# Norms of latents and latent keys by one float32 product over 512 tokens in a two-layer decoder trunk

## The chip, the cores and the metric

One core of one Trainium2 chip runs the whole program in one launch. The metric is the time of the run on the device in microseconds (us), where less is better.

## What is computed

The reference is a trunk of two layers (`D_MODEL` 1024, 512 tokens, float32). A layer mixes tokens by latent attention (MLA, 4 heads) and by stick-breaking attention (4 heads), gates and merges the two, and ends with a gated MLP. The change touches the root-mean-square norms of MLA:

```python
def rms_norm(x, g):
    x32 = x.astype(jnp.float32)
    y = x32 * lax.rsqrt(jnp.mean(x32 * x32, axis=-1, keepdims=True) + EPS)
    return (y * g.astype(jnp.float32)).astype(x.dtype)
...
        q = (rms_norm(q_lat, g_q_lat[l]) @ w_uq[l]).reshape(b, s, MLA_HEADS, QK_HEAD_DIM)
        kv = (rms_norm(kv_lat, g_kv_lat[l]) @ w_ukv[l]).reshape(b, s, MLA_HEADS, QK_NOPE_DIM + V_HEAD_DIM)
        k_nope, v_mla = kv[..., :QK_NOPE_DIM], kv[..., QK_NOPE_DIM:]
        k_rope_h = jnp.broadcast_to(k_rope[:, :, None, :], (b, s, MLA_HEADS, QK_ROPE_DIM))
        k = jnp.concatenate([k_nope, k_rope_h], axis=-1)
        q = rms_norm(q, g_q_head[l])
        k = rms_norm(k, g_k_head[l])
```

There are two norms of latents in a layer (256 query features, 128 key-value features) and one norm of the keys for each of four heads: six in a layer, twelve in all, that the change rewrites. The norms of the queries of each head and those of the residual stream stay as they were.

## The kernel before, in words

Features lie along the 128 partitions and the 512 tokens along the columns, so a norm needs a sum over partitions, which a product with ones gives. A weight product is three products of `fp32r` operands (`mm3`: high by high, high by low, low by high), each a 128x128 block of weights against 512 columns of activations. `split` makes such a pair of parts from a float32 tile: a copy on ScalarE, a difference on VectorE.

The program is first listed in the order of the data flow (`Program.add`), with an estimated duration for each instruction. `Program.order` then simulates the engines: each takes the most urgent instruction whose operands and memory are there. The result is a fixed order for each engine, and each engine works through its own order without overtaking. Urgency is the place in the data flow plus a bias. A list of `fills` (24 products each: projections of stick-breaking heads, and gates) serves to keep TensorE at work while the norms and softmaxes run on ScalarE and VectorE: two of them are listed ahead of `latents` with a low urgency (`BIAS_F`), the others come out of `weave`, one for every four steps of the two attentions.

A norm before (`rsqrt_cols`, then `across`): `sums` takes four products, each with a 128x128 block of squares as weights and one column of ones as the moving side, into a [128 tokens, 4] corner of a PSUM bank. Six operations follow on [128, 4] tiles (Ln and Exp on ScalarE, four on VectorE, a Newton step among them). `across` then brings the factor back into every partition by four products, a spread column as weights against the identity. In `latents` VectorE reads that bank directly; for the keys in `mla_proj` ScalarE copies it to `rks` first. The sum of squares of the shared rotary key is taken once a layer by four products of 64 rows (`rsum`), and each head adds it on its [128, 4] tile.

In layer 0 a wide form, `norm_wide`, serves the norm of the input: one float32 product of a 128x128 block of ones with 512 columns gives the sum in every partition, and Ln, Exp and four VectorE operations work on 128x512 tiles.

```python
            r = across(rsqrt_cols(sq, div, 0))          # latents
        rks = slot()                                    # mla_proj
        act(rks, across(rsqrt_cols(sqk, QK, 0, rsum)), AF.Copy)
```

Of the kernel before, what the change touches and what calls it, by code (L numbers as in the profile page):

```python
# [13 lines left out]
ALU = mybir.AluOpType  # L14
# [17 lines left out]
# columns of the packed per-feature vectors  # L32
# [11 lines left out]
class View:  # L44
    """a part of a tile that gets its memory when the order of the program is known"""
# [48 lines left out]
class Program:  # L94
    """Instructions in the order of the data flow; run() picks the order of issue: each engine takes the
    most urgent instruction whose operands and memory are there, by estimated durations."""
# [13 lines left out]
    def add(self, eng, name, cost, table=None, writes=(), reads=(), alt=None, **kw):  # L110
        o = Op()
        o.alt, o.taken = alt, False
        o.eng, o.name, o.kw, o.cost, o.table = eng, name, kw, cost, table
        o.seq = len(self.ops)
        o.prio = o.seq + self.bias
        o.succ, o.slots, o.need = [], [], set()
        for v, w in [(v, False) for v in reads] + [(v, True) for v in writes]:
            t = v.t
            whole = self.tags[t.tag]["psum"]
            for q, qw, qp, qc in t.log:  # L120
                if not (w or qw) and (not whole or q.eng == eng):
                    # two engines do not read one bank of PSUM at a time
                    continue
                if whole or (qp[0] < v.p[1] and v.p[0] < qp[1] and qc[0] < v.c[1] and v.c[0] < qc[1]):
                    if q is not o:
                        o.need.add(q)
            if w and not whole:
                t.log = [e for e in t.log
                         if not (v.p[0] <= e[2][0] and e[2][1] <= v.p[1] and v.c[0] <= e[3][0] and e[3][1] <= v.c[1])
                         or e[0] is o]  # L130
            t.log.append((o, w, v.p, v.c))
            if not t.users or t.users[-1] is not o:
                t.users.append(o)
            if t not in o.slots:
                o.slots.append(t)
        self.ops.append(o)

    def order(self):
# [44 lines left out]
        # the tensor engine's clock halves after a mostly idle window  # L183
# [22 lines left out]
        while events:  # L206
# [19 lines left out]
            for name, e in engines.items():  # L226
                while e["free"] <= time:
# [16 lines left out]
                    # a far more urgent instruction that is about to be ready goes first  # L244
# [22 lines left out]
            # an engine that is still busy looks again when its instruction ends  # L267
# [35 lines left out]
# tiles of features around a norm that are worked in halves of the tokens  # L303
# [14 lines left out]
# steps of the later adaLN products beside each kind of unit  # L318
# [3 lines left out]
class Unit:  # L322
    """both parts of the weights of one step: eight blocks of 128 columns, in two halves"""
# [10 lines left out]
def trunk_kernel(ctx, tc, keys, xT, wstream, wada, cols, cvec, pos, freqs, out):  # L334
# [14 lines left out]
    # ------------------------------------------------------------ instructions  # L349
# [3 lines left out]
    def act(o, i, func, scale=None, bias=None, accum=None, alone=False):  # L353
# [18 lines left out]
        if accum is None and not alone and func in (AF.Copy, AF.Identity):  # L372
            # a copy, scaled and shifted: VectorE can do it too
            akw = dict(out=o, in0=i, scalar1=1.0 if scale is None else scale, scalar2=bias, op0=ALU.mult)
            if bias is not None:
                akw["op1"] = ALU.add
            alt = ("dve", "tensor_scalar", 66 + (1.041 if is_psum(i) or is_psum(o) else 0.52) * o.n
                   + 60 * (len(reads) - 1), akw)
# [21 lines left out]
    def mm(o, w, r, start, stop, skip=False):  # L400
        n = o.n
        # a short product does not hide the load of the next weights
        cost = max(n / 2.4, 107.0) if r.dt == F32R else max(4 * n / 2.4, 215.0)
        kw = dict(out=o, lhsT=w, rhs=r, start=start, stop=stop)
        if skip:
            kw["skip_group_check"] = True
        R.add("pe", "matmul", cost + 3, None, [o], [w, r], **kw)
# [7 lines left out]
    # ------------------------------------------------------------ constants  # L415
# [39 lines left out]
    for n in range(2):  # L455
        # the row in every partition
# [6 lines left out]
    def make_masks():  # L463
# [4 lines left out]
        masks["causal"] = rounded(scr)          # [q, k]: k <= q stays  # L468
        select(scr, zer, ALU.is_gt, NEG, 1, -1)
        masks["strict"] = rounded(scr)          # [k, q]: k < q stays  # L470
        masks["neg"] = rounded(negm)
        select(scr, negm, ALU.is_ge, 0.0, -1, 1)
        masks["tri"] = rounded(scr)             # [j', j]: -1 where j' >= j

    # ------------------------------------------------------------ norms
    def sums(sq):
        """[128 tokens, blocks]: the sums over the rows"""
# [6 lines left out]
    def rsqrt_cols(sq, div, eps, more=None):  # L484
        """[128 tokens, blocks] of 1 / sqrt((sum over the rows + more) / div + eps), with a Newton step"""
        t = sums(sq)
        n = t.n
        if more is not None:
            u = small(n)
            tt(u, t, more, ALU.add)  # L490
            t = u
# [9 lines left out]
    def across(col):  # L501
        """[128, tokens] with the value of its token in every row"""
# [5 lines left out]
    def split(src):  # L508
        """src as the sum of two parts that one pass each carries exactly"""
# [5 lines left out]
    def square(acc, k, x, c=slice(0, S)):  # L515
        """adds the square of feature tile k to the sum"""
# [10 lines left out]
    def norm_wide(acc):  # L527
        """the same in fewer steps, with more work for each"""
        ps = bank()
        mm(ps, ones, acc, True, True)  # L530
        r, v, q = slot(), slot(), slot()
        act(r, ps, AF.Ln, scale=1.0 / D, bias=epsc[:, 0:1])
        act(r, r, AF.Exp, scale=-0.5)
        ts(v, ps, -0.5 / D, ALU.mult, -0.5 * EPS, ALU.add)
        tt(q, r, r, ALU.mult)
        tt(q, q, v, ALU.mult)
        stt(r, q, 1.5, r, ALU.add, ALU.mult)
        return r
# [14 lines left out]
    # ------------------------------------------------------------ halves of the tokens  # L553
    HALF = (slice(0, S // 2), slice(S // 2, S))

    def residual(xs, tiles, prods, gate, acc):
        """the last tiles of a residual sum, in two halves of the tokens, so that the norm of one half runs beside
        the products of the other; gives 1 / rms of the first, and a function for that of the second"""
# [18 lines left out]
    def grouped(l, i, xs, r, later, blocks, banks, kk=KC):  # L577
        """products of the first features of h, feature by feature and in halves of the tokens"""
        h = [pair() for _ in range(kk)]
        for n in range(2):  # L580
            c = HALF[n]
            for k in range(kk):
# [3 lines left out]
                for g, ps in enumerate(banks):  # L586
                    w, b = blocks(g, k)
                    # where the first half is not complete, its first product has cleared the bank
# [4 lines left out]
    # ------------------------------------------------------------ adaLN  # L593
    def ada_tile(l, m):
        """mod[128 m ..] = b_ada + c_act w_ada, the features of c along the rows"""
# [30 lines left out]
    # ------------------------------------------------------------ weight stream  # L626
# [15 lines left out]
    # ------------------------------------------------------------ products  # L642
# [12 lines left out]
    # ------------------------------------------------------------ rotary tables  # L655
    def rope_tables():
        # 32 frequencies for four blocks of tokens along the rows
# [24 lines left out]
    # ------------------------------------------------------------ attention  # L682
    def latents(l, us):
        cl = colt[l]
        lat = []
        for grp, div in (((0, 1), 256), ((2,), 128)):
# [6 lines left out]
            r = across(rsqrt_cols(sq, div, 0))  # L693
# [4 lines left out]
        # the shared rotary key, without the norm, which every head applies to its scores  # L698
        t, u = slot(), slot()
        act(t[0:64], us[3][0:64], AF.Square)  # L700
        rsum = small(4)
        act(rsum, sums(t[0:64]), AF.Copy)
# [5 lines left out]
        return lat, rsum, split(t)  # L708

    def packed():  # L710
        """views for four blocks of width 512 - 128 j, both parts, in five slots"""
# [13 lines left out]
    def mla_proj(l, hd, lat, rsum, heads):  # L725
# [17 lines left out]
        rks = slot()  # L743
        act(rks, across(rsqrt_cols(sqk, QK, 0, rsum)), AF.Copy)
# [11 lines left out]
        # the scale of the scores is in it: (sum / QK + EPS) * QK under the root  # L756
        rqs = rsqrt_cols(sqn, 1.0, 1)
        if hd % 2 == 0:
            # the values of two heads, two blocks of tokens to a bank
# [64 lines left out]
    def sb_evac(l, hd, n, ps, bqs, res):  # L824
        """queries and keys, or, with the tokens along the rows, values of a stick-breaking head"""
# [16 lines left out]
    def sb_head(hd, res, ys):  # L842
# [4 lines left out]
        for J in (0, 1, 3, 2):  # L847
            z = zv[J]
            b = slice(J * P, J * P + P)
            # block 3 shares the bank of block 1, whose first product has cleared it  # L850
# [44 lines left out]
    # ------------------------------------------------------------ gates and branches  # L895
# [26 lines left out]
    # ------------------------------------------------------------ one layer  # L922
    def layer(l, xs, xsrc, first, r=None, later=None):
        cl = colt[l]
        # latents and the first heads of stick-breaking, over the features of h as they come
        nb = 7 if l else 8
        if l == 0:
# [3 lines left out]
            r = norm_wide(acc)  # L931
# [31 lines left out]
        # products of h alone, which fill the gaps of the chains  # L963
# [27 lines left out]
        lat, rsum, krh = latents(l, us)  # L991

        def latent():
            yield from mla_proj(l, 0, lat, rsum, heads)
            for hd in range(NH):
                if hd + 1 < NH:
                    yield from mla_proj(l, hd + 1, lat, rsum, heads)
# [126 lines left out]
    # ------------------------------------------------------------ issue  # L1124
# [39 lines left out]
def _unit(key, i):  # L1164
    """[128, 1024]: the weights that one step of the program takes from the stream"""
# [82 lines left out]
```

## Time and profile before

| | |
|---|---|
| median of 3 runs | 1482.76 us |
| lowest, highest | 1479.37, 1483.85 us |
| profiled execution | span 1478.3 us; the page gives no other time of that execution |
| PE busy | 1452.6 us (98%) |
| PEld (weight loads) | 1233.1 us (83%) |
| DVE (VectorE) busy | 1003.2 us (68%) |
| ACT (ScalarE) busy | 662.6 us (45%) |
| POOL (GpSimd) busy | 28.5 us (2%), all of it before 75 us |
| DMA | 185 MB, mean 125 GB/s |

PE is TensorE's products, PEld its loads of weights, which run beside them. A float32 product shows as two records of PE and two of PEld; an `fp32r` product shows as one of each. Ends of products are modelled, so the distance from one start to the next says more than a duration. Line 1154 is the one line that issues nearly every instruction: groups are told apart by tiles (`s` a working tile, `sm` a small one, `ps` a PSUM bank, `raw` a streamed weight tile, `c` a constant) and by shapes.

### The profile page before, as it was taken

The numbers are of one execution on the slowest core, as the hardware profiler recorded it, in microseconds if no ns is written. First come the engines' busy times: TensorE is split into PE (matmuls) and PEld (weight loads), VectorE is DVE, ScalarE is ACT, GpSimd is POOL, SyncE is SP. The second block draws the span as 40 slices with busy tenths as digits, with TensorE's granted clock in tenths as the row PEclk, the third lists the DMA queues.
The fourth block names the chain that finished last, engine by engine and source line by source line (L and its number), as shares of the span: only waits on it lengthen the run. The fifth ranks groups of instructions, "written<-read, shape, count | busy, mean of one in ns | idle before, by whom it ended". The sixth has DMA issues, their size and how long they took to land.

```text
span 1478.3 us, 19625 instructions
## 1 busy us (share of the span) xinstructions
PE 1452.6 (98%) x7322; PEld 1233.1 (83%) x7322; DVE 1003.2 (68%) x2026; ACT 662.6 (45%) x1210; POOL 28.5 (2%) x30
## 2 busy tenths in 40 slices
PE   5899999999999999999999999999999999999998
PEld 3688888888988888888898888888889888888887
DVE  8986789856699977877265666834629775356631
ACT  4476685433444423344145676833415443233410
POOL 3300000000000000000000000000000000000000
PEclk9999999999999999999999999999999999999999
DMA  9321147854256676534230112432602433332311
GB/s 341 117 70 38 57 129 268 273 178 163 86 184 208 221 242 214 182 92 153 81 100 28 38 44 72 134 109 86 200 1 88 141 95 119 90 95 76 114 39 43
DMA packets 68209, 185.13 MB, mean 125 GB/s; under 512 B 7697, under 2 KB 8081, under 8 KB 68114
## 3 DMA queue, kind: packets, MB, share of 16 engines
q1 hardware_dynamic: 67968, 183.74, 39.0%
q8 instruction: 57, 0.93, 0.3%
q14 instruction: 38, 0.31, 0.1%
q10 hardware_dynamic: 146, 0.15, 0.0%
HBM read 179.66 MB, written 4.19 MB: 124 GB/s over the span
## 4 chain that ended last, share of the span: by engine, by line
PE 96%; DVE 2%; ACT 1%; issue 0%; DMA 0%; POOL 0%; SPq 0%; DVEq 0%; ACTq 0%
PE ps L1154 96%; DVE s L1154 2%; DMA s<-in_xT_dram 0%; ACT s L1154 0%; ACT c L1154 0%; POOL s L1154 0%; DVE c L1154 0%; SPq L1154 0%; DVEq L1236 0%; DVE sm L1154 0%; DVEq L1154 0%; ACT L1149 0%; ACTq L1154 0%
## 5 line engine op out<-in xcount | busy, mean ns | idle before, releaser
L1154 PE MATMUL ps<-s,s 128*128 128x512 f32 (+2 forms) x6660 | 1414.9, 370 | 12.4 <-ACT s L1154 11.4
L1154 PEld LDWEIGHTS ps<-s,s 128*128 128x128 f32 x6660 | 1159.9, 189 | 222.6 <-ACT s L1154 14.8
L1154 DVE TENSOR_TENSOR s<-raw,s 128x512 fp32r<-128x512 f32 (+1 forms) x458 | 300.9, 681 | 169.3 <-ACT s L1154 87.4
L1154 ACT ACTIVATE s<-raw 128x512 fp32r<-128x512 f32 (+1 forms) x407 | 244.8, 623 | 376.6 <-PE ps L1154 256.4
L1154 ACT ACTIVATE s<-s 128x512 f32<-128x512 f32 (+4 forms) x325 | 189.3, 595 | 184.0 <-DVE s L1154 179.4
L1154 DVE SCALAR_TENSOR_TENSOR s<-ps,c,s 128x510 f32<-128x510 f32 (+4 forms) x249 | 175.5, 728 | 127.1 <-PE ps L1154 111.3
L1154 DVE TENSOR_TENSOR s<-s,s 128x512 fp32r<-128x512 f32 (+4 forms) x266 | 172.7, 654 | 36.2 <-ACT s L1154 28.9
L1154 ACT ACTIVATE s<-ps,c 128x512 f32<-128x512 f32 (+1 forms) x135 | 95.3, 733 | 88.7 <-PE ps L1154 88.1
L1154 DVE CUSTOM_DVE_ANT_0 s<-s,c,sm 128x512 f32<-128x512 f32 x96 | 79.3, 833 | 6.2 <-DMA s<-in_wada_dram 3.1
L1154 DVE CUSTOM_DVE_ANT_0 s<-s,c,c 128x512 f32<-128x512 f32 x96 | 73.2, 769 | 13.3 <-DMA s<-in_wada_dram 12.7
L1154 ACT ACTIVATE s<-ps 128x512 f32<-128x512 f32 (+4 forms) x126 | 68.2, 557 | 30.6 <-PE ps L1154 29.1
L1154 PE MATMUL ps<-c,s 128*128 128x1 f32 (+2 forms) x312 | 55.7, 239 | 0.0
L1154 DVE TENSOR_SCALAR s<-raw 128x512 fp32r<-128x512 f32 (+2 forms) x67 | 27.3, 413 | 41.0 <-PE ps L1154 35.2
L1154 PEld LDWEIGHTS ps<-c,s 128*128 128x128 f32 (+1 forms) x312 | 47.2, 175 | 4.4 <-DVE s L1154 0.4
L1154 ACT ACTIVATE s<-s,c 128x256 fp32r<-128x256 f32 (+2 forms) x56 | 27.5, 526 | 41.7 <-DVE s L1154 41.3
L1154 PE MATMUL ps<-s,c 128*128 128x128 f32 (+3 forms) x162 | 41.8, 317 | 4.2 <-DVE s L1154 4.2
L1154 DVE SCALAR_TENSOR_TENSOR s<-s,c,s 128x256 fp32r<-128x256 f32 (+1 forms) x64 | 34.4, 564 | 1.2 <-ACT s L1154 0.9
L1154 PEld LDWEIGHTS ps<-s,c 128*128 128x128 f32 x162 | 28.8, 191 | 6.6 <-DVE s L1154 5.8
L1154 DVE TENSOR_SCALAR s<-ps,c 128x512 f32<-128x512 f32 (+1 forms) x26 | 20.2, 779 | 20.7 <-PE ps L1154 17.9
L1154 ACT ACTIVATE s<-s,sm,sm 128x128 f32<-128x128 f32 (+3 forms) x32 | 20.8, 649 | 17.6 <-DVE sm L1154 17.6
L1154 DVE TENSOR_TENSOR s<-ps,s 128x512 fp32r<-128x512 f32 (+1 forms) x40 | 24.6, 634 | 4.9 <-ACT s L1154 4.6
L1154 DVE SCALAR_TENSOR_TENSOR s<-s,c,ps 128x256 f32<-128x256 f32 (+1 forms) x54 | 25.4, 506 | 3.3 <-PE ps L1154 3.2
(54 smaller groups left out, 302.5 us busy)
## 6 DMA issues: line engine op xcount, KB each, us to landing
raw<-in_wstream_dram SPq DMA_DIRECT2D x221, 512.0 KB, 3.8
s<-in_wada_dram SPq DMA_DIRECT2D x192, 256.0 KB, 4.0
raw<-in_wstream_dram SPq DMA_DIRECT2D x12, 448.0 KB, 3.4
s<-in_xT_dram SPq DMA_DIRECT2D x16, 256.0 KB, 3.9
keep<-s SPq DMA_DIRECT2D x8, 256.0 KB, 2.0
s<-keep SPq DMA_DIRECT2D x8, 256.0 KB, 3.9
out_dram<-s SPq DMA_DIRECT2D x8, 256.0 KB, 2.0
raw<-in_wstream_dram SPq DMA_DIRECT2D x4, 320.0 KB, 3.4
```

What stands on the lines that cost most here:

```text
L1154: getattr(engines[o.eng], o.name)(**kw)
```

## The change

`norm_wide` becomes `rsqrt_wide(sq, div)`, with any divisor and three VectorE operations in place of four, and the twelve norms of latents and keys use it. `rsum` goes: the squares of the shared rotary key are kept as a tile and added to those of a head by one operation on 64 rows. The result of `rsqrt_wide` lies in SBUF, so the copy to `rks` goes as well. Comments were removed too, which shifts line 1154 to 1148 and nothing else.

```diff
-    def rsqrt_cols(sq, div, eps, more=None):
+    def rsqrt_cols(sq, div, eps):
         t = sums(sq)
         n = t.n
-        if more is not None:
-            u = small(n)
-            tt(u, t, more, ALU.add)
-            t = u
...
-    def norm_wide(acc):
+    def rsqrt_wide(sq, div):
         ps = bank()
-        mm(ps, ones, acc, True, True)
-        r, v, q = slot(), slot(), slot()
-        act(r, ps, AF.Ln, scale=1.0 / D, bias=epsc[:, 0:1])
+        mm(ps, ones, sq, True, True)
+        r, q = slot(), slot()
+        act(r, ps, AF.Ln, scale=1.0 / div, bias=epsc[:, 0:1])
         act(r, r, AF.Exp, scale=-0.5)
-        ts(v, ps, -0.5 / D, ALU.mult, -0.5 * EPS, ALU.add)
-        tt(q, r, r, ALU.mult)
-        tt(q, q, v, ALU.mult)
+        stt(q, ps, div * EPS, r, ALU.add, ALU.mult)
+        stt(q, q, -0.5 / div, r, ALU.mult, ALU.mult)
         stt(r, q, 1.5, r, ALU.add, ALU.mult)
         return r
...
-            r = across(rsqrt_cols(sq, div, 0))
+            r = rsqrt_wide(sq, div)
...
-        rsum = small(4)
-        act(rsum, sums(t[0:64]), AF.Copy)
+        rsq = t[0:64]
...
-        rks = slot()
-        act(rks, across(rsqrt_cols(sqk, QK, 0, rsum)), AF.Copy)
+        tt(sqk[0:64], sqk[0:64], rsq, ALU.add)
+        rks = rsqrt_wide(sqk, QK)
...
-            r = norm_wide(acc)
+            r = rsqrt_wide(acc, D)
```

Since the order is computed anew, instructions move on every engine. Three places follow.

TensorE, norms of the latents of layer 0, before: the four products of `across` for the query latents (`ps_794`), those for the key-value latents (`ps_813`) and the four of the rotary key (`ps_798`) alternate; `ps_717` and `ps_726` are the two fills, and `ps_839` is the first product of a head with a normed latent.

```order
L1154 MATMUL ps_726<-s_235,s_637 128x512
L1154 MATMUL ps_794<-c_82,sm_751 128x128
L1154 MATMUL ps_798<-c_76,s_784 128x1
L1154 MATMUL ps_794<-c_82,sm_751 128x128
...
L1154 MATMUL ps_813<-c_82,sm_767 128x128
L1154 MATMUL ps_717<-s_351,s_599 128x512
...
L1154 MATMUL ps_726<-s_295,s_626 128x512
L1154 MATMUL ps_839<-s_829,s_652 128x512
```

The same place now: the products with ones for both latents (`ps_719`, `ps_729`, weights `c_76`), transposes of a value tile (`ps_735`), the two fills (`ps_713`, `ps_752`) to their ends, and only then the first products with normed latents (`ps_850`, `ps_852`, moving tiles `s_843` and `s_856`).

```order
L1148 MATMUL ps_278<-s_599,s_607 128x512
L1148 MATMUL ps_719<-s_710,c_76 128x512
L1148 MATMUL ps_729<-s_697,c_76 128x512
L1148 MATMUL ps_735<-c_82,s_725 128x128
L1148 MATMUL ps_713<-s_199,s_601 128x512
...
L1148 MATMUL ps_752<-s_599,s_640 128x512
L1148 MATMUL ps_850<-s_843,s_651 128x512
L1148 MATMUL ps_852<-s_843,s_651 128x512
L1148 MATMUL ps_850<-s_856,s_651 128x512
```

Before, the last product of the fill `ps_726` stood 236 rows behind the first product of a head; now both fills end ahead of it, in the 55 rows between the products with ones and `ps_850`.

ScalarE at the same place, before: the table of Ln and Exp is loaded behind the last evacuation (`s_742`), and the operations on small tiles follow.

```order
L1154 ACTIVATE s_735<-s_689 128x512
L1154 ACTIVATE s_742<-ps_279,sm_97 128x512
L1149 ACT_TABLE_LOAD
L1154 ACTIVATE sm_751<-ps_730,c_78 128x4
L1154 ACTIVATE sm_767<-ps_747,c_78 128x4
```

Now five more operations that need no table stand ahead of the load (`s_731`, `s_738`, `s_754`, `s_761`, `s_767`), and Ln and Exp work on 128x512 tiles.

```order
L1148 ACTIVATE s_745<-ps_278,sm_97 128x512
L1148 ACTIVATE s_754<-ps_735 128x512
L1148 ACTIVATE s_761<-s_745 128x512
L1148 ACTIVATE s_767<-s_721 128x512
L1143 ACT_TABLE_LOAD
L1148 ACTIVATE s_771<-ps_729,c_78 128x512
L1148 ACTIVATE s_791<-ps_719,c_78 128x512
L1148 ACTIVATE s_771<-s_771 128x512
```

The load of the table, and with it Ln, has moved behind work that came after it before.

VectorE at the same place now: the three operations of either norm in turn, then the latents times their factors (`s_834`, `s_840`, `s_846`) and the low parts.

```order
L1148 SCALAR_TENSOR_TENSOR s_803<-ps_729,s_771 128x512
L1148 SCALAR_TENSOR_TENSOR s_808<-ps_719,s_791 128x512
L1148 SCALAR_TENSOR_TENSOR s_803<-s_803,s_771 128x512
L1148 SCALAR_TENSOR_TENSOR s_808<-s_808,s_791 128x512
L1148 SCALAR_TENSOR_TENSOR s_771<-s_803,s_771 128x512
L1148 SCALAR_TENSOR_TENSOR s_791<-s_808,s_791 128x512
L1148 SCALAR_TENSOR_TENSOR s_834<-s_677,c_90,s_771 128x512
L1148 SCALAR_TENSOR_TENSOR s_840<-s_682,c_90,s_771 128x512
L1148 SCALAR_TENSOR_TENSOR s_846<-s_687,c_90,s_791 128x512
L1148 TENSOR_TENSOR s_856<-s_834,s_843 128x512
```

Six wide operations stand where small ones stood, ahead of everything that the heads wait for.

## Rows read from the trace of the kernel before

**Rows 1.** Page, part 4: chain that ended last, shares by engine.

```profile
PE 96%; DVE 2%; ACT 1%; issue 0%; DMA 0%; POOL 0%; SPq 0%; DVEq 0%; ACTq 0%
```

**Rows 2.** The same chain in order of time: start us, us, what.

```profile
59.21 32.53 PE ps L1154 x152
...
93.99 1378.80 PE ps L1154 x7026
```

**Rows 3.** Windows: stretch, length, busy us of PE, PEld, DVE, ACT, POOL, PEclk, DMA.

```profile
300.00:325.00 25.00, 25.00 (x112) 20.71 (x111) 13.71 (x26) 7.94 (x14) 0.00 (x0) 1.00 0.45 144
94.00:225.00 131.00, 131.00 (x768) 115.14 (x769) 100.52 (x258) 96.41 (x200) 0.00 (x0) 1.00 0.25 78
225.00:300.00 75.00, 75.00 (x339) 62.13 (x338) 69.08 (x160) 36.43 (x62) 0.00 (x0) 1.00 0.79 270
780.00:950.00 170.00, 170.00 (x986) 148.64 (x984) 116.23 (x287) 117.85 (x243) 0.00 (x0) 1.00 0.19 55
```

**Rows 4.** Timeline of PE, norms in layer 0: start us, us, operation, records.

```profile
77.50 0.28 PE L1154 MATMUL ps<-c,s 128*128 128x1 f32 x2
...
77.95 1.65 PE L1154 MATMUL ps<-c,s 128*128 128x1 f32 x16
79.46 0.48 PE L1154 MATMUL ps<-s,s 128*128 128x512 f32 x1
...
82.61 0.38 PE L1154 MATMUL ps<-c,s 64*128 64x1 f32 x2
82.92 0.49 PE L1154 MATMUL ps<-c,sm 128*128 128x128 f32 x2
...
86.01 0.48 PE L1154 MATMUL ps<-s,s 128*128 128x512 f32 x1
86.33 0.38 PE L1154 MATMUL ps<-c,sm 128*128 128x128 f32 x2
86.47 6.39 PE L1154 MATMUL ps<-s,s 128*128 128x512 f32 x27
...
97.35 0.47 PE L1154 MATMUL ps<-c,sm 128*128 128x128 f32 x2
97.65 0.28 PE L1154 MATMUL ps<-c,s 128*128 128x1 f32 x2
97.80 0.47 PE L1154 MATMUL ps<-c,sm 128*128 128x128 f32 x2
```

**Rows 5.** Windows with a single group of products: the norm of the input, four fp32r products.

```profile
56.80:59.00 2.20, 2.08 (x4) 1.16 (x4) 2.17 (x3) 1.06 (x3) 2.20 (x2) 0.50 0.00 0
11.80:14.00 2.20, 2.07 (x2) 0.50 (x2) 2.20 (x8) 0.55 (x1) 0.00 (x0) 1.00 1.03 389
```

**Rows 6.** Groups by form: line engine op, shapes, count | busy us, mean ns | idle.

```profile
L1154 ACT ACTIVATE s<-ps,c 128x512 f32<-128x512 f32 x125 | 88.5, 737 | 88.7 <-PE ps L1154 88.1
L1154 ACT ACTIVATE s<-s 128x512 f32<-128x512 f32 x138 | 86.7, 630 | 100.5 <-DVE s L1154 97.7 <-DMA s<-in_xT_dram 1.4
L1154 ACT ACTIVATE s<-ps 128x512 f32<-128x512 f32 x69 | 40.8, 594 | 21.6 <-PE ps L1154 21.1
L1154 DVE SCALAR_TENSOR_TENSOR s<-ps,s 128x512 f32<-128x512 f32 x16 | 11.0, 688 | 6.0 <-ACT s L1154 5.9
L1154 DVE SCALAR_TENSOR_TENSOR s<-s,s 128x512 f32<-128x512 f32 x1 | 1.6, 1632 | 0.0
L1154 DVE TENSOR_TENSOR s<-s,s 64x512 f32<-64x512 f32 x8 | 5.4, 677 | 1.3 <-ACT s L1154 1.3
L1154 DVE TENSOR_TENSOR sm<-sm,sm 128x4 f32<-128x4 f32 x20 | 3.1, 157 | 0.3
```

**Rows 7.** Timeline, norm of the input and table load: start us, us, engine, operation.

```profile
14.79 0.69 DVE L1154 TENSOR_SCALAR s<-ps 128x512 f32<-128x512 f32 x1 [0.26 <-ACT s L1154]
...
16.02 3.00 POOL L1154 TENSOR_TENSOR s<-raw,s 128x512 fp32r<-128x512 f32 x2 [14.59 <-ACT s L1154]
...
79.00 1.28 ACT L1149 ACT_TABLE_LOAD   x1
```

More of the change, by code (lines that the diff above doesn't have):

```diff
@@ L707, in latents @@
         tt(t, t, u, ALU.add)
-        return lat, rsum, split(t)
+        return lat, rsq, split(t)
     def packed():
@@ L723, in flip, with mla_proj @@
         R.add("pe", "transpose", 60.0, None, [o], [i, ident], out=o, in_=i, identity=ident)
-    def mla_proj(l, hd, lat, rsum, heads):
+    def mla_proj(l, hd, lat, rsq, heads):
         cl = colt[l]
@@ L990, in layer @@
             fill(BIAS_F)
-        lat, rsum, krh = latents(l, us)
+        lat, rsq, krh = latents(l, us)
         def latent():
-            yield from mla_proj(l, 0, lat, rsum, heads)
+            yield from mla_proj(l, 0, lat, rsq, heads)
             for hd in range(NH):
                 if hd + 1 < NH:
-                    yield from mla_proj(l, hd + 1, lat, rsum, heads)
+                    yield from mla_proj(l, hd + 1, lat, rsq, heads)
                 yield from mla_attend(hd, heads, krh, ys)
```

## The prediction

> **What bounds the kernel now.** I read the chain that ended last first, by engine and then in order of time. TensorE holds 96% of it [rows 1], and from 93.99 us on there is one unbroken piece of 1378.80 us with 7026 products [rows 2]: nothing that another engine does is on the path there, and what counts is how much TensorE has to do and whether it keeps being fed. [...]
>
> So a saved TensorE microsecond is a saved microsecond, and work added on VectorE and ScalarE costs nothing until TensorE waits for it.
>
> **The change, part by part.**
>
> *Products removed.* I go by distances between starts, since the durations overlap. The products of `sums`: 16 records, eight products, take from 77.95 to 79.46 us, 0.19 us a product [rows 4]. The products of `across`: between two products of 512 columns, one takes 0.14 us (86.33 to 86.47), and the 512 columns ahead of it take 0.32 instead of 0.223 us (86.01 to 86.33), together 0.24 us. Alternating, one of each kind takes 0.45 us (97.35 to 97.80). Four of each in a norm are 4 x 0.45 = 1.80 us, and by the two separate prices 4 x 0.19 + 4 x 0.24 = 1.72 us. Upper bound: `across` at its whole duration of 0.38 us, 2.28 us. I take 1.80 us, measured for the mix that the norms really issue. Twelve norms: 21.6 us.
>
> [...]
>
> *Products added.* One float32 product of 512 columns per norm. The trace has one on 128 rows, at the norm of the input: two records, 2.07 us. [...] I take 0.89 us, since all twelve stand in stretches where TensorE is never idle; 10.7 us in all.
>
> *The rotary key's sum.* Four products of 64 rows in each layer go. One took 0.31 us among products of `across` (82.61 to 82.92), the other kind of sum 0.19 us; at 0.25 us, eight are 2.0 us (1.5 to 2.5).
>
> TensorE together: 21.6 - 10.7 + 2.0 = 12.9 us less.
>
> *VectorE and ScalarE.* Per norm VectorE gets three operations on 128x512 in place of four of 0.16 us, five for keys [rows 6]. The one on PSUM is 0.69 us. The two on SBUF have only the one row of that form, 1.63 us, but there GpSimd worked beside it [rows 7], and GpSimd has nothing after 75 us; so 0.69 us. With 0.68 us per head for the 64-row addition, a layer adds 6 x 2.07 + 4 x 0.68 - 2 x 0.63 - 4 x 0.79 = 10.7 us. ScalarE adds per norm 0.74 + 0.63 us for Ln and Exp less some 0.46 us for the small ones, and loses the copy of 0.59 us per head: about 3 us a layer. The gaps in layer 0 are 30.5 and 34.6 us, in layer 1 53.8 and 52.1 us [rows 3]. Covered as a sum; that cover is thinner as a chain.
>
> *The chain.* A norm hands its factor on at about the old time: two wide passes on ScalarE (1.37 us) and three on VectorE (2.07 us) stand against small operations, four more products and, for keys, a copy. The two latents go side by side, so one waits for the other's operation at each step. In layer 0 the order also puts five ScalarE operations (some 3.1 us) ahead of the table load that Ln needs. Counting those from the load's end in the old run (80.28 us) [rows 7], I get the first high part of a normed latent at about 91.2 us and its low part at 92.6. TensorE, from 77.5 us [rows 4], has two products with ones, some 50 of 512 columns and a few short ones ahead of the first head, 13.5 us, and gets there at 91.0. So it waits 0 to 2 us. In layer 1 no table load intervenes: about 10 us of products against a chain of 8.6. The products with ones for keys stand 12 rows behind the squares' source, 2.3 us of products against some 2 us of Square and addition; a few tenths each. I add 2 us in all (0 to 10), and keep the upper end for the range.
>
> *The norm of the input.* It loses one VectorE operation of 0.69 us [rows 7] in a stretch where the chain runs on VectorE: 0.7 us less (0 to 1.5).
>
> Sum: 1478.3 - 12.9 + 2.0 - 0.7 = 1466.7 us as a span. The page gives no more of that execution than its span; the median of the runs, 1482.8, is 4.5 us longer, which I leave as it is: **1471 us**, 0.8% faster. A measurement of this kernel can tell about 0.3%, 4.4 us, from no change.
>
> **The rivals.**
>
> *A: TensorE waits for the norms (slower).* Both fills are spent before the first head of a layer, and the orders then show head 0's projections, the product with ones, its sums and values in a row with no fill for some 60 rows, where before a fill ran through that place. TensorE takes its order as it stands, so one late factor stops everything behind it. For it: the two latents were about even in my count above, and VectorE runs at 77% in 94 to 225 us, where each added 0.7 us operation can queue ahead of a part that TensorE needs. Against it: a key's factor is used only by VectorE after the scores, never by TensorE. It decides from 13.6 us of waits, what the rest saves: 1.1 us per norm cancels it. At 3 us for each pair of latents and 2 us for each of eight heads it is 22 us: 1491 us.
>
> *B: VectorE's added work comes out behind layer 0 (no change).* If the 10.7 us do not fit into gaps of the attention, they push into 225 to 300 us, where VectorE has 5.9 us left [rows 3] and makes low parts of weights for TensorE. Layer 0 then gives back 4.8 to 10.7 us: 1476 to 1482 us. Against it: layer 0's attention had 30.5 us of gaps.
>
> *C: the wide product costs what the one row says (no change).* At 2.07 us, twelve are 24.8 us against 23.6 us removed: with the waits and the input norm 1485 us. [...]
>
> *D: the removed products were nearly free (slower).* If the short products hid wholly beside the weight loads of their neighbours, only the 10.7 us of wide products and the 2 us of waits would be left, less 0.7 us: 1495 us. The 16 records that alone took 1.51 us, and the stretched product beside another (0.32 for 0.223 us), speak against it. [...]
>
> **How the numbers follow.** Forecast 0.70; A 0.10; B 0.11; C 0.06; D 0.03. The forecast's own range is 1462 (2.28 us per norm removed, 0.85 us added, no waits: 17.2 + 2.5 + 1.5 us less) to 1478 (1.72 us removed, 8 us of waits). Most of the forecast, and the half of B that ends below 1478.3, is faster by over 0.3%: 0.73. Within 0.3%: the rest of B, C and the forecast's edge, 0.15. Slower: A, D and the edge of C, 0.12. For eight in ten the range takes in B: 1462 to 1483.
>
> **What would show it.** In the changed profile: the chain still one unbroken TensorE piece from about 94 us; two records per product with ones of some 0.45 us from start to start at a granted clock of 1.00; 112 products in 25 us as before in the MLP; TensorE busy less by 11 to 15 us; VectorE busy up by about 21 us, ScalarE by about 6. Wrong if the waits list gains entries of TensorE on VectorE or ScalarE of more than a few us, above all at the first product of head 0 in either layer (A), if stretches of 225 to 300 us show fewer products than before (B), or if the wide product takes 2 us (C).

## The result, and the profile after

The changed kernel takes **1470.0 us** (median of 5 runs, 1469.88 to 1470.24) against 1482.76 us (1479.37 to 1483.85): a ratio of 0.9922, 95% interval 0.991 to 0.9933. Forecast were 1471.0 us and a range of 1462 to 1483. The median fell by 12.8 us, the span of the profiled execution by 9.8 us, from 1478.3 to 1468.5. The two differ because the times of the kernel before lie in two groups, near 1479.5 and near 1483.5 us, its profiled execution in the lower one, while all times of the changed kernel lie together, 1.5 us above its span. The comparison of spans is therefore the one to explain.

The page of the changed kernel, parts 1 and 4:

```profile
PE 1441.6 (98%) x7138; PEld 1213.9 (83%) x7138; DVE 1020.5 (69%) x2011; ACT 666.5 (45%) x1202; POOL 28.5 (2%) x30
PE 93%; DVE 3%; ACT 2%; DMA 1%; issue 1%; POOL 1%; SPq 0%; DVEq 0%; POOLq 0%; ACTq 0%
```

TensorE is busy 11.0 us less (1452.6 before), VectorE 17.3 us more (1003.2), ScalarE 3.9 us more (662.6). TensorE's share of the chain went from 96% [rows 1] to 93%. The chain in order of time (start us, us, what) shows where the three points went: about one of them ahead of 76.73 us, where the path now runs over a transfer and ScalarE (before, it ran over TensorE from 59.21 us on [rows 2]), the others at the first heads of the layers:

```profile
72.18 4.51 ACT s L1148 x8
76.73 13.95 PE ps L1148 x59
90.72 3.28 PE ps L1148 x11
94.02 0.61 ACT s L1148
94.65 3.27 DVE s L1148 x5
97.97 1.94 PE ps L1148 x14
99.93 3.77 ACT s L1148 x8
104.05 1.16 ACT s L1148 x2
105.23 2.02 DVE s L1148 x3
107.29 695.33 PE ps L1148 x3576
...
802.65 1.76 ACT s L1148 x3
...
807.17 4.20 PE ps L1148 x28
811.40 3.87 ACT s L1148 x8
815.29 1.64 ACT s L1148 x3
816.98 71.02 PE ps L1148 x398
...
888.78 575.25 PE ps L1148 x2762
```

The one piece from 93.99 us on [rows 2] is broken in two places: from 94 to 107 us and from 802 to 817 us, the places of those heads (a third break, at 888 us, takes 0.8 us). There the path runs through ScalarE and VectorE, whose turns the norms share with squares, evacuations of PSUM and low parts. The first product with a normed latent of layer 0 starts at 90.72 us after a wait of 0.04 us: the waits stand behind it, inside the first head. The windows that answer to [rows 3], with one more over nearly the whole rest of the program (stretch, length, busy us of PE, PEld, DVE, ACT, POOL, PEclk, DMA):

```profile
300.00:325.00 25.00, 25.00 (x112) 20.71 (x111) 12.21 (x21) 9.78 (x16) 0.00 (x0) 1.00 0.47 141
94.00:225.00 131.00, 129.56 (x721) 110.42 (x721) 108.98 (x259) 104.13 (x209) 0.00 (x0) 1.00 0.27 83
225.00:300.00 75.00, 75.00 (x336) 62.24 (x335) 66.56 (x155) 35.77 (x59) 0.00 (x0) 1.00 0.83 273
780.00:950.00 170.00, 168.75 (x918) 143.18 (x918) 132.88 (x293) 127.81 (x251) 0.00 (x0) 1.00 0.22 67
94.00:1463.00 1369.00, 1366.31 (x6864) 1159.80 (x6864) 936.15 (x1853) 615.95 (x1111) 0.00 (x0) 1.00 0.38 121
```

From 94 us to the end TensorE now waits 1369.00 - 1366.31 = 2.7 us; before it did not wait. The MLP streams as before (112 products in 25 us), and behind layer 0's attention VectorE is not fuller (66.56 of 75 us, 69.08 before). The two wide products of the latents in layer 0, and the norm of the input (timelines: start us, us, operation, records):

```profile
76.73 1.98 PE L1148 MATMUL ps<-s,c 128*128 128x512 f32 x4
78.55 0.27 PE L1148 MATMUL ps<-c,s 128*128 128x128 f32 x1
```

```profile
15.13 0.69 DVE L1148 SCALAR_TENSOR_TENSOR s<-ps,s 128x512 f32<-128x512 f32 x1 [0.73 <-ACT s L1148]
15.85 3.32 DVE L1148 SCALAR_TENSOR_TENSOR s<-s,s 128x512 f32<-128x512 f32 x2
```

Four records take 78.55 - 76.73 = 1.82 us, 0.91 us a product. GpSimd was busy from 15.70 to 18.63 us, beside the two operations that took 3.32 us. From 75 us on, where it has no instruction, the same form took 679 ns (24 operations); in the groups by form, over the whole program, the added VectorE operations are these:

```profile
L1148 DVE SCALAR_TENSOR_TENSOR s<-ps,s 128x512 f32<-128x512 f32 x29 | 19.5, 682 | 10.1 <-ACT s L1148 10.1
L1148 DVE SCALAR_TENSOR_TENSOR s<-s,s 128x512 f32<-128x512 f32 x26 | 19.1, 753 | 0.1
```

### The profile page after: what moved, and what is told of

Same layout as the page of the kernel before. It is cut to its first block, busy times and chain, and to the rows that moved or that the text cites. A ratio compares the mean times of both kernels' runs of the same rounds, so it can differ in the third digit from the quotient of the medians.

```text
span 1468.5 us, 19218 instructions
## 1 busy us (share of the span) xinstructions
PE 1441.6 (98%) x7138; PEld 1213.9 (83%) x7138; DVE 1020.5 (69%) x2011; ACT 666.5 (45%) x1202; POOL 28.5 (2%) x30
## 4 chain that ended last, share of the span: by engine, by line
PE 93%; DVE 3%; ACT 2%; DMA 1%; issue 1%; POOL 1%; SPq 0%; DVEq 0%; POOLq 0%; ACTq 0%
PE ps L1148 93%; DVE s L1148 2%; ACT s L1148 2%; DMA raw<-in_wstream_dram 1%; POOL s L1148 1%; ACT c L1148 0%; DMA s<-in_xT_dram 0%; SPq L1148 0%; POOLq L1230 0%; DVEq L1230 0%; DVE c L1148 0%; DVE sm L1148 0%; DVEq L1148 0%; ACTq L1148 0%; ACT L1143 0%
## 5 line engine op out<-in xcount | busy, mean ns | idle before, releaser
L1148 ACT ACTIVATE s<-s 128x512 fp32r<-128x512 f32 (+4 forms) x339 | 197.1, 597 | 184.6 <-DVE s L1148 179.7
L1148 DVE CUSTOM_DVE_ANT_0 s<-s,c,sm 128x512 f32<-128x512 f32 x96 | 79.4, 835 | 6.2 <-DMA s<-in_wada_dram 3.2
L1148 PE MATMUL ps<-s,c 128*128 128x128 f32 (+3 forms) x186 | 55.0, 348 | 4.8 <-DVE s L1148 3.7
L1148 DVE TENSOR_SCALAR s<-ps,c 128x512 f32<-128x512 f32 (+1 forms) x38 | 29.6, 780 | 39.6 <-PE ps L1148 34.2
L1148 PEld LDWEIGHTS ps<-s,c 128*128 128x128 f32 x186 | 33.8, 191 | 11.1 <-DVE s L1148 5.7
L1148 PE MATMUL ps<-c,s 128*128 128x128 f32 (+1 forms) x200 | 40.2, 247 | 0.3 <-DVE s L1148 0.3
L1148 DVE SCALAR_TENSOR_TENSOR s<-s,c,s 128x256 fp32r<-128x256 f32 (+1 forms) x70 | 38.3, 577 | 1.0 <-ACT s L1148 0.7
L1148 PEld LDWEIGHTS ps<-c,s 128*128 128x128 f32 x200 | 29.4, 162 | 3.6 <-ACT s L1148 1.5
L1148 DVE SCALAR_TENSOR_TENSOR s<-ps,s 128x512 f32<-128x512 f32 (+1 forms) x37 | 22.8, 625 | 10.2 <-ACT s L1148 10.1
L1148 DVE TENSOR_TENSOR s<-s,ps 128x512 f32<-128x512 f32 x32 | 21.8, 683 | 9.6 <-PE ps L1148 9.6
L1148 POOL TENSOR_TENSOR s<-raw,s 128x512 fp32r<-128x512 f32 x16 | 25.3, 1599 | 36.4 <-ACT s L1148 36.4
```

The costliest lines, as they stand in the source:

```text
L1148: getattr(engines[o.eng], o.name)(**kw)
```

## Experiments

Times are medians, ratios are against the kernel before on the same chip. The most telling view is two windows of 50 us in which the first heads of the two layers stand, 75 to 125 us and 800 to 850 us. The kernel before, and the changed kernel:

```profile
75.00:125.00 50.00, 49.89 (x292) 43.65 (x291) 39.35 (x99) 36.13 (x78) 0.00 (x0) 1.00 0.15 48
800.00:850.00 50.00, 50.00 (x290) 43.64 (x289) 34.31 (x84) 32.70 (x70) 0.00 (x0) 1.00 0.13 38
```

```profile
75.00:125.00 50.00, 48.45 (x240) 37.90 (x239) 44.99 (x96) 41.33 (x82) 0.00 (x0) 1.00 0.14 48
800.00:850.00 50.00, 49.09 (x265) 41.17 (x264) 42.67 (x93) 38.75 (x81) 0.00 (x0) 1.00 0.17 48
```

VectorE fills 45.0 of 50 us where it filled 39.4, and 42.7 where it filled 34.3. TensorE waits 1.6 and 0.9 us. The granted clock stays at 1.00.

### The kernel before, again

The unchanged kernel, for the clock that is listed with each of its times.

> The kernel before once more, so that its runs, which lie at 1479.4 to 1483.9 us, show span and clock for each. Theory of products: the stretch from 94 us on is the same in all of them, and a difference of 4 us can only come from the clock in the first 94 us; the clock listed with the longer runs is then lower by about 0.003. Rival: the clock is the same in all, and the 4 us come from something else.

1480.47 us, ratio 0.9998 (0.9987 to 1.0009), span 1478.0 us. The clock differs as the theory said: it is 0.995 or 0.996 at 1482.39 us and above, 0.997 or 0.998 at 1480.91 us and below. Where in the program the longer ones lose it is not shown, since the profile is of one of the shorter.

### Latents by columns, and keys by columns

```diff
-            r = rsqrt_wide(sq, div)
+            r = across(rsqrt_cols(sq, div, 0))
```

> The changed kernel with the four norms of the latents by columns again, keys wide. Theory of products: four norms give back 4 x 0.91 = 3.6 us, so 1473.6 us, less what the waits ahead of head 0 cost (up to 2.7 us): 1471 to 1473.6 us. Rival, waits: the wide latents cost more in waits than their products save, and this kernel is faster than the changed one, under 1469.5 us.

1468.46 us, ratio 0.9914 (0.99 to 0.9928), span 1466.9 us. Undoing the change for the latents does not cost the products that come back; it gains 1.5 us. The second layer's waits are gone, and VectorE has 4.7 us more room there:

```profile
75.00:125.00 50.00, 48.78 (x268) 40.67 (x267) 44.32 (x100) 37.30 (x79) 0.00 (x0) 1.00 0.16 52
800.00:850.00 50.00, 50.00 (x272) 42.42 (x271) 38.01 (x84) 35.53 (x73) 0.00 (x0) 1.00 0.13 38
```

The size of the gain is less certain than its sign. Near 60 us, ahead of all norms of the attention, the granted clock falls for a while: the windows 56 to 60 and 60 to 64 us have 0.54 and 0.61 in the kernel before, 0.51 and 0.64 in the changed kernel, 0.65 and 0.92 in this run, 1.7 us less lost than in the changed kernel; this run's TensorE then waits 0.7 us for VectorE at the first sums, so at most 1.0 of the 1.5 us can come from there. What is safe is that the wide latents gain nothing on top of wide keys.

The other half, keys back, wide latents kept:

```diff
-        tt(sqk[0:64], sqk[0:64], rsq, ALU.add)
-        rks = rsqrt_wide(sqk, QK)
+        rks = slot()
+        act(rks, across(rsqrt_cols(sqk, QK, 0, rsq)), AF.Copy)
...
```

> The changed kernel with the eight norms of keys by columns again and the rotary key's sum once a layer, latents wide. Theory of products: 8 x 0.91 + 2.0 = 9.3 us back, 1479 us. Rival, waits: the keys' wide norms also add waits, so undoing them gives back less, 1475 us or under.

1476.4 us, ratio 0.9968 (0.9956 to 0.9979), span 1475.1 us: between the two expectations. By spans against the kernel before, wide keys alone give 11.4 us, wide latents alone 3.2 us, and both together 9.8 us (each with the new norm of the input). The parts do not add up: on top of wide latents the keys give 6.6 us, on top of wide keys the latents take 1.6. About 1.0 us in each of the three gains lies behind the last product (5.0 us to the end before, 4.1 after), and in the two halves up to 1.7 us in the clock near 60 us (here 0.60 and 0.98 in the two windows). So the keys carry the gain, and the latents add nothing to it.

### The new product twice, and in one pass

Each of the twelve wide products is issued twice.

```diff
+        if twice:
+            mm(ps, ones, sq, True, True)
         mm(ps, ones, sq, True, True)
...
```

> The changed kernel with each of the twelve wide products issued twice into the same bank. Theory of products: 12 x 0.91 = 10.9 us more, 1481 us, TensorE busy up by 10.9 us. Rival: part of the products stands where TensorE waits anyway, and the second copy costs half or less, under 1475.5 us. Rival C of the prediction: 2.07 us each, 1495 us.

1474.43 us, ratio 0.9954 (0.994 to 0.9968), 4.4 us for 10.3 us of products (12 x 0.86, two records of 0.43 us each): the rival's half or less. TensorE is busy 5.9 us more, not 10.9. From 94 us on TensorE's waits fell from 2.7 to 0.1 us, so 2.6 us of the copies stand where it waited. That leaves some 3.3 us that I cannot place; the order of the other products differs too. So I took products away instead:

```diff
-        mm(ps, ones, sq, True, True)
+        mm(ps, ones if div == D else ones.as_(F32R), sq, True, True)
...
-            sq = slot()
+            sq = slot(dt=F32R)
...
-        sqk = slot()
+        sqk = slot(dt=F32R)
...
```

> The changed kernel, but the squares of the twelve norms are rounded to fp32r and the product with ones is one fp32r product of 512 columns instead of a float32 one; the sums differ by that rounding. Theory (the wide product is four passes at the high clock, and stands on TensorE's path): from start to start it falls from 0.86 us (two records of 0.43) to 0.22 us, 12 x 0.64 = 7.7 us less than the changed kernel's 1470.0: 1462.3 us, one record per product. Rival (the wide products stand partly where TensorE would wait anyway, as the second copies seemed to, which cost 4.4 us for 10.3): half of it or less, 1466 us or above, and the waits on VectorE and ScalarE in the heads 0 grow.

1470.14 us, ratio 0.9916 (0.9902 to 0.9929), span 1469.1 us: **nothing gained** over the changed kernel, which is beyond what the rival gave. The windows, first the two of 50 us, then finer ones:

```profile
75.00:125.00 50.00, 46.15 (x224) 38.23 (x224) 43.68 (x94) 40.38 (x80) 0.00 (x0) 0.93 0.15 46
800.00:850.00 50.00, 47.51 (x246) 40.92 (x245) 40.26 (x88) 36.75 (x77) 0.00 (x0) 0.93 0.17 48
```

```profile
75.00:96.00 21.00, 18.96 (x85) 14.51 (x84) 17.66 (x31) 18.79 (x33) 0.00 (x0) 1.00 0.21 65
96.00:100.00 4.00, 2.89 (x16) 2.61 (x17) 4.00 (x7) 4.00 (x10) 0.00 (x0) 0.86 0.00 0
100.00:104.00 4.00, 4.00 (x16) 3.71 (x17) 3.55 (x10) 2.88 (x8) 0.00 (x0) 0.50 0.00 0
104.00:108.00 4.00, 4.00 (x16) 3.10 (x16) 2.06 (x4) 3.01 (x6) 0.00 (x0) 0.79 0.00 0
```

The saved products came back twice. TensorE waits 3.85 and 2.49 us where it waited 1.55 and 0.91, 3.9 us more. And after those waits the granted clock falls to 0.50: 0.14 x 4 + 0.50 x 4 + 0.21 x 4 = 3.4 us of full speed lost in layer 0, and 0.07 x 50 = 3.5 us in layer 1. Together 10.8 us, more than the 7.7 us saved. In turn the clock near 60 us loses 1.7 us of full speed here and 3.4 us in the changed kernel (windows 56 to 60 and 60 to 64 us: 0.74 and 0.84 against 0.51 and 0.64). That makes 9.1 - 7.7 = 1.4 us more, against spans that differ by 0.6 us; the rest I leave open. No single wait from 75 us on was longer than 1.3 us, and the clock fell once in each layer.

### The old products twice

In the kernel before, the eight short products of each of the twelve norms are issued twice.

```diff
-            mm(ps[:, i:i + 1], sq[:, i * P:i * P + P], ones[0:n, 0:1], True, True)
+            for _ in range(times):
+                mm(ps[:, i:i + 1], sq[:, i * P:i * P + P], ones[0:n, 0:1], True, True)
...
-            mm(ps[:, i * P:(i + 1) * P], col[:, i:i + 1].spread(P), ident, True, True)
+            for _ in range(times):
+                mm(ps[:, i * P:(i + 1) * P], col[:, i:i + 1].spread(P), ident, True, True)
...
```

> The kernel before, with each of the short products of its twelve norms (four sums, four across) issued twice. Theory (1.80 us per norm on TensorE's path): 12 x 1.80 = 21.6 us more than the kernel before, about 1502 us. By the starts in the changed profile, where 104 short records of layer 0 went and the layer became only 3.4 us shorter, I hold less to be as likely: 89 and 113 ns a record, 192 records, 19 us, 1500 us. Rival (short products hide beside their neighbours): 8 us or less, below 1490 us.

1511.35 us, ratio 1.0192 (1.0178 to 1.0206), span 1509.8 us, 31.5 us more: above every expectation. The windows in which the clock was below 1.00, two finer ones around one fall, and the products that TensorE issued there (start us, us, operation, records):

```profile
75.00:100.00 25.00, 24.31 (x127) 21.48 (x125) 16.54 (x35) 13.32 (x26) 0.00 (x0) 0.80 0.20 63
...
150.00:175.00 25.00, 25.00 (x154) 22.90 (x153) 15.12 (x41) 11.80 (x26) 0.00 (x0) 0.93 0.13 43
800.00:825.00 25.00, 25.00 (x155) 23.28 (x154) 11.31 (x27) 10.68 (x22) 0.00 (x0) 0.86 0.07 22
825.00:850.00 25.00, 24.70 (x145) 22.02 (x143) 19.58 (x47) 16.95 (x37) 0.00 (x0) 0.89 0.09 22
850.00:875.00 25.00, 25.00 (x137) 21.79 (x137) 10.56 (x31) 9.84 (x21) 0.00 (x0) 0.97 0.17 53
...
804.00:812.00 8.00, 8.00 (x65) 7.74 (x64) 5.46 (x11) 6.91 (x12) 0.00 (x0) 1.00 0.23 68
812.00:824.00 12.00, 12.00 (x70) 11.41 (x71) 4.84 (x15) 2.89 (x9) 0.00 (x0) 0.72 0.00 0
```

```profile
810.59 6.47 PE L1156 MATMUL ps<-c,s 128*128 128x1 f32 x42
```

TensorE is busy nearly throughout, yet the clock falls in stretches with many short products, here (1.00 to 812 us, 0.72 in the 12 us behind) where a row of 42 records of one column stands: 0.20 + 0.07 + 0.14 + 0.11 + 0.03, times 25 us, are 13.75 us of full speed. Near 60 us the kernel before loses 3.4 us, 1.7 us more than this run, whose mean clock over the span is 0.990, so the clock makes up 12.1 us of the difference. Without that, 31.5 - 12.1 = 19.4 us remain, 1.6 us a norm where I took 1.80. That the removed products were nearly free (rival D) is out.

### VectorE: a longer chain, and work beside it

```diff
         stt(r, q, 1.5, r, ALU.add, ALU.mult)
+        if div != D:
+            for _ in range(3):
+                ts(r, r, 1.0, ALU.mult)
```

> The changed kernel with three more multiplications by one on VectorE, 128x512 from SBUF to SBUF, some 0.45 us each, at the end of each of the twelve factors: each chain is 1.35 us longer. Theory (only the two latent norms at the first head of a layer have TensorE waiting, the keys' factors have time): 1.35 to 2.7 us per layer, 1473 to 1475 us, with the added waits at the first head of each layer. Rival 1 (TensorE waits for every factor): 12 x 1.35 = 16 us, 1486 us. Rival 2 (the order moves other products ahead and hides it): 1471 us or less.

1480.86 us, ratio 0.9996 (0.9987 to 1.0004), 10.9 us more than the changed kernel: between the theory and rival 1, and the whole gain of the change is gone.

```profile
75.00:125.00 50.00, 45.66 (x205) 36.04 (x204) 43.48 (x97) 36.39 (x73) 0.00 (x0) 0.90 0.14 44
800.00:850.00 50.00, 46.86 (x235) 38.35 (x234) 44.34 (x100) 35.36 (x72) 0.00 (x0) 0.93 0.16 48
```

The waits stand around the first heads, where the theory put them, 2.8 and 2.2 us more than in the changed kernel, above its 1.35 to 2.7 us a layer only in the first. Not all of them are waits for latents: one of 1.7 us, at 113 us, is for a low part that VectorE makes behind operations of a later key's norm, so the keys' factors do not quite have time either. What the theory left out is the clock: 0.10 x 50 + 0.07 x 50 = 8.5 us of full speed. Waits and clock together, 13.5 us, are more than the 10.9 us measured; what makes up for the difference is open. And with work that no chain contains:

```diff
         stt(r, q, 1.5, r, ALU.add, ALU.mult)
+        if div != D:
+            d = slot()
+            for _ in range(3):
+                tt(d, r, r, ALU.mult)
```

> The changed kernel with three more additions of work on VectorE per norm, 128x512 products of SBUF tiles of 0.69 us each into a tile that nobody reads: 12 x 2.07 = 24.8 us of VectorE work that no chain contains. Theory (VectorE's gaps in the attention cover it): within 2 us of the changed kernel, 1468 to 1472 us. Rival (VectorE is near its limit beside the norms; added work comes out as waits of TensorE or behind the attention): half of it or more, 1482 us or above.

1488.03 us, ratio 1.0037 (1.0023 to 1.005), 18.0 us more: the rival. The two windows, and VectorE at the latents' products:

```profile
75.00:125.00 50.00, 41.62 (x188) 31.97 (x187) 44.89 (x84) 32.82 (x63) 0.00 (x0) 0.93 0.12 38
800.00:850.00 50.00, 42.50 (x200) 33.94 (x199) 45.79 (x95) 33.39 (x68) 0.00 (x0) 0.93 0.12 33
```

```profile
87.06 0.69 DVE L1152 TENSOR_TENSOR s<-s 128x512 f32<-128x512 f32 x1
87.67 0.75 DVE L1152 SCALAR_TENSOR_TENSOR s<-s,c,s 128x512 f32<-128x512 f32 x1
...
92.50 0.75 DVE L1152 SCALAR_TENSOR_TENSOR s<-s,c,s 128x512 f32<-128x512 f32 x1
```

VectorE is no fuller than in the changed kernel in the first window (44.89 of 50 us): what is added pushes everything behind it. TensorE waits 6.8 and 6.6 us more, and the clock loses another 7.0 us. Two causes are mixed here, and no run separates them: a VectorE with no room left, and its fixed order. The added products are listed at each norm, so the order puts them among the latents' own products: in the changed kernel these follow one another from 88.44 us on, within 2.07 us, and here the last of the three starts 4.83 us behind the first. Work that no chain contains still stands in front of work that one does.

### Where TensorE keeps being fed, one pass pays

First with the latents by columns, which leave no waits in layer 1; only the keys' products are single passes (against the run with the latents by columns):

```diff
-        mm(ps, ones, sq, True, True)
+        mm(ps, ones if div == D else ones.as_(F32R), sq, True, True)
...
-        sqk = slot()
+        sqk = slot(dt=F32R)
...
```

> The run with the latents by columns as before and the keys wide, but the keys' eight products with ones are fp32r products on squares rounded to fp32r. Theory (in the run with one pass for all twelve, 7.7 us of saved products came back as waits at the heads 0 and as two stretches of 6.8 us at half the clock behind them; the latents by columns leave no such waits, so the clock stays up): 8 x 0.64 = 5.1 us less than the 1468.5 of the run with float32 products for the keys, 1463.4 us, with a granted clock of 1.00 from 75 us on. Rival (VectorE and ScalarE bound the attention as a whole, wherever TensorE saves): 1467 us or above, with waits of TensorE that grow by 3 us or more.

1463.84 us, ratio 0.9883 (0.9869 to 0.9896): 4.6 of the 5.1 us, and the clock is 1.00 in both windows (0.999 over the whole span).

```profile
75.00:125.00 50.00, 48.38 (x270) 41.27 (x269) 43.25 (x98) 39.98 (x82) 0.00 (x0) 1.00 0.19 63
800.00:850.00 50.00, 50.00 (x277) 43.24 (x277) 38.57 (x86) 38.22 (x79) 0.00 (x0) 1.00 0.15 39
```

Then all twelve as single passes, with two more projections of h to fill the waits (against the run with one pass):

```diff
-FILLS = 2
+FILLS = 4
```

> The run with one fp32r pass for all twelve products with ones, and FILLS at 4 instead of 2: two more projections of h that depend on no norm may stand beside the latents and head 0. Theory (the lack of products that are ready is what costs the waits, and the waits cost the clock): no stretch at half the clock after 75 us, waits after 75 us under 2 us, and the 7.7 us of saved products show: 1460 to 1463 us. Rival (VectorE has to prepare the fills' weights in the same stretch and hands the factors on later): waits and half-clock stretches remain, 1468 us or above.

1461.42 us, ratio 0.9869 (0.9853 to 0.9885), 8.7 us less than the same products with two fills.

```profile
75.00:125.00 50.00, 46.65 (x235) 37.80 (x234) 43.65 (x85) 37.82 (x73) 0.00 (x0) 1.00 0.21 64
800.00:850.00 50.00, 49.78 (x276) 43.02 (x275) 40.13 (x87) 37.37 (x76) 0.00 (x0) 1.00 0.15 46
```

The second layer hardly waits, and the clock stays up in both layers. In the first the theory was wrong in part: 3.35 us of waits remain, but they stand elsewhere: 2.8 us of them, at 76.5 and 79.4 us, are waits for ScalarE ahead of the norms of the latents, not at the first head. The four fills with the float32 products:

> The changed kernel with FILLS at 4 instead of 2. Theory (the 2.7 us of waits at the heads 0 are a lack of ready products): they go, 1467 to 1468 us. Rival (VectorE's work on the fills' weights delays the factors): no gain, 1470 us or above.

1470.12 us, ratio 0.9925 (0.9913 to 0.9938): no gain. Waits for ScalarE of 1.0 and 1.7 us at 77 and 80 us came in the place of those at the first head, and the clock was 0.97 in the window from 75 to 125 us. So fills help one pass, not the float32 form. Both runs with four fills have the wait of 1.7 us near 78 us; the clock fell behind it in this one alone, and why is open.

Last, the six half norms of the residual sums in the same form, one pass over 256 columns, on top of the four fills:

```diff
-        return across(rsqrt_cols(acc, D, 0))
+        return rsqrt_wide(acc, D)
...
-        mm(ps, ones if div == D else ones.as_(F32R), sq, True, True)
-        r, q = slot(), slot()
+        mm(ps, ones.as_(sq.dt), sq, True, True)
+        r, q = slot()[:, 0:sq.n], slot()[:, 0:sq.n]
...
-        acc = slot()
+        acc = slot(dt=F32R)
...
```

> The run with one fp32r pass and FILLS at 4, and the six half norms of the residual sums (256 columns each) in the same form, on squares rounded to fp32r. Theory (their short products stand on TensorE's path too): by the starts, four records of sums at 89 ns and four of across at 113 ns go, 0.81 us, and one product of 256 columns, 0.13 us, comes: 6 x 0.68 = 4.1 us less than 1461.4, 1457.3 us. Rival (their factor is waited for between the residual sum and the next products, and wide passes on ScalarE and VectorE hand it on later): TensorE waits behind the residual sums, where it never did before, and the time is 1461 us or above.

1457.73 us (1455.89 to 1458.4), ratio 0.9831 (0.9816 to 0.9846): 3.7 of the 4.1 us. TensorE's waits over the whole program add up to 23.3 us, against 23.2 us in the run with one pass and four fills, so the residual sums added none to speak of; from 75 to 125 us it is busy 47.66 of 50 us at a granted clock of 0.97. It is the fastest version, 12.3 us under the changed kernel. Its sums of squares are of squares rounded to `fp32r`, so it trades some accuracy of the norms, which the changed kernel does not.

## Why the prediction held, and where it did not

- **Bound.** That a saved TensorE microsecond is a saved one held for the change itself, and for 4.6 of 5.1 and 3.7 of 4.1 us later. It is not general: 7.7 us saved at the same place gave nothing with two fills, and 8.7 us with four.
- **Products removed, 1.80 us a norm.** High; this is the term of the sum that was off. The doubled products give 1.6 us once the clock is taken out, and so does the change itself, (11.0 + 10.7 - 2.0) / 12; my lower bound was 1.72. I had read the distances between starts where these products crowd together [rows 4], which may be why.
- **Product added, 0.89 us.** No run shows this figure itself, nor the 0.85 us of the range: 0.89 was my estimate, four times the 0.223 us from one `fp32r` product to the next (112 in 25.00 us [rows 3]). The runs showed 0.91 us in the open, at a granted clock of 1.00, and 0.86 us, two records of 0.43, in the run with the product twice. So the term was about right, and rival C, 2.07 us, is out. The 1.00 beside the 2.07 us [rows 5] was no reading: the clock's records in that trace begin 25.6 us after the start, so at what clock that product ran is not shown.
- **TensorE together, 12.9 us.** It was 11.0 us, at the edge of the 11 to 15 told. These 1.9 us, with 0.7 us more of waits and 0.3 us less at the norm of the input, are 2.9 us, of which 1.0 us came back where the sum had nothing: from the last product to the end it took 5.0 us before and 4.1 after. What is left is about the 1.8 us by which the sum's span, 1466.7 us, fell short of 1468.5. That the median came within 1 us is luck: the 4.5 us between median and span, which I left as it was, became 1.5.
- **Waits, 2 us.** 2.7 us, all but 0.3 at the first heads of both layers, as told. The sign told for a right forecast, one unbroken chain from 94 us on, was too strict for a sum that itself had 2 us of waits.
- **VectorE and ScalarE covered.** It held for the change, with less added than told (17.3 and 3.9 us for about 21 and 6), but for a reason that does not carry. I added up gaps over 131 and 170 us [rows 3]. The cover that counts is at the first heads, where VectorE is busy 45 of 50 us: the added operations fit just about, and 24.8 us more of them cost 18.0 us. Rival B was looked for in the wrong place, behind the attention, where VectorE got emptier.
- **Rival A.** The place and the mechanism were right, the price was not: the waits came to 2.7 us, not 22. The runs show how near it was: 1.35 us more a chain took back 10.9 us.
- **Sizes on VectorE.** 0.68 us for the operation on two SBUF tiles from 75 us on, 0.69 taken (by duration; four in a row take 2.49 us, some 0.6 us from start to start); the mean of 753 ns takes in two of 1.65 us. At the norm of the input, where GpSimd works beside, these two took 3.32 us, as the 1.63 us row said [rows 6, 7], so the operation behind them started at 19.21 us in place of 19.60, 0.4 us earlier and not 0.7.

## What to carry to other kernels

When TensorE is the bound, count what it saves, and then look at the narrowest 50 us of the engine that takes over the work, not at its sum of gaps. A product moved off TensorE pays while other products are ready to take its place; where they are not, the wait costs its own length and can cost the clock too (with one pass and two fills, 3.9 us of added waits and 6.9 us of full speed for 7.7 us saved; a chain 1.35 us longer, 10.9 us), so here fills and short chains came before smaller products. Take each half of a change by itself: here the keys, whose factor only VectorE uses, carried the gain, and the latents, whose factor TensorE's next products need, added nothing to it.

## What the hardware showed that I had not expected

The granted clock fell with no wait in sight: in the run with the short products twice, TensorE was busy 8.00 of 8 us with 65 products from 804 to 812 us and 12.00 of 12 us from 812 to 824 us, and the clock of that second window is 0.72, 3.4 us of full speed lost. A row of 42 records of one column each stands there, from 810.59 us on. In that run the short products cost more than their time: some 12 us of full speed, against some 19 us for the products themselves. That the short products are the cause rests on this one run; in the kernel before, with half as many of them, the clock stayed at 1.00 from 75 us to 1476 us. In the runs with waits, each short (1.3 us at the longest in the one-pass run, 3.4 us with the work beside), the clock fell behind them, but by no fixed price: 6.9 us of full speed against 3.9 us of added waits with one pass, 8.5 against 5.0 with the longer chain, 7.0 against 13.4 with the work beside, and nothing in the changed kernel with its 2.7 us.
